# Scores of a two-branch encoder: a head's two maps alternate on the halves of TensorE's rows, and a 64-row product is padded with zeros to 128 rows

## The chip, the cores and the metric

The kernel runs on one core of one Trainium2 chip. The metric is device time of one execution in microseconds (us), the median of three runs. TensorE (PE) multiplies, VectorE (DVE) and ScalarE (ACT) do the elementwise work, GpSimd (POOL) and SyncE (SP) mostly issue transfers.

## The reference

Two encoder layers over 256 tokens of 2048 features, float32. Per layer, with `h = rmsnorm(x)`:

```
# differential attention, 8 heads, two maps c per head, 64 dims each
scores = einsum('bqhcd,bkhcd->bhcqk', qb, kh) * scale
probs = softmax(scores)
weights = probs[:, :, 0] - lam * probs[:, :, 1]
...
# latent attention, 8 heads: 128 plain dims, and 64 rotated dims whose key all heads share
scores = (einsum('bqhd,bkhd->bhqk', qn, k_nope) + einsum('bqhr,bkr->bhqk', qr, k_rope)) * scale
probs = softmax(scores)
...
x = x + (sigmoid(ga) * y_diff + sigmoid(gb) * y_mla) @ w_out
x = x + swiglu(rmsnorm(x))
x = x + sigmoid(rmsnorm(x) @ w_ple_gate) * (p @ w_ple_in)
```

The rest of the layer is matrix products with 2048 x 2048 or larger weights.

## The kernel before

Every operand of a product is held in two parts: the leading bits (`hi`) and the exact rest (`lo`); three products of parts make one product of values. The tokens lie along the free axis, 256 of them, so an operand tile is [128 features, 256 leading | 256 rest]. Weights come from HBM in pieces of up to 8 blocks of 128 x 128 (`piece`): SP issues the load, ACT writes `whi`, DVE writes `wlo`, and PE uses both; three buffers of each exist. A large product (`emit`) does per 128 features one matmul of 512 columns and one of 256 (L199, L200), or three of 256 (L195 to L197).

Scores are made by `scores` (L317 to L322) in a PSUM bank `S` of [128 queries, 2 query blocks, 256 keys]; `ps_s` has two banks. For each query block the query part is the stationary operand and the key part streams 256 columns, for the three pairs of parts that `three` lists. In the differential branch the two maps of a head share a tile: map 0 on partitions 0 to 63, map 1 on 64 to 127, so a matmul uses 64 of the array's 128 rows: 12 of them per head, 6 for each map (`diff_weights`). In the latent branch (`mla_weights`) a score block is three matmuls on all 128 rows (`qn`, `kn`) and three on 64 rows (`qr`, `kr`): two heads share a `qr` tile, one on each half of the partitions, and the shared rotated key `kr` lies twice in its tile, once on each half. So a latent head is 3 + 3 + 3 + 3 matmuls, 6 of them on 64 rows.

`exps` then takes the bank: DVE finds the row maxima (L327), ACT the exponents (L330) and DVE the inverse sums. The heads are pipelined: the weights of head h+1 are traced before the output of head h, and between them stand steps of other products (`beside`, or the first gates). The order on each engine is not that of the source: the Tile scheduler orders instructions by its own timeline simulation when the program is built, so the pieces of a score block can lie apart, with rows of other products between them.

Of the kernel before, what the change touches and what calls it, by code (L numbers as in the profile page):

```python
# [12 lines left out]
F32 = mybir.dt.float32  # L13
F32R = mybir.dt.float32r
# [5 lines left out]
P = 128  # L20
# [30 lines left out]
def encoder(ctx, tc, x, p, positions, cols, lams, wq, wk, wv, wcq, wckv, wkr, wga, wgb,  # L51
# [27 lines left out]

    # Operands of products: [128 features, leading bits of 256 tokens | rest]  # L80
    ua = [const.tile([P, 2 * T], F32R, name=f"ua{j}") for j in range(NC)]
    ub = [const.tile([P, 2 * T], F32R, name=f"ub{j}") for j in range(NC)]

    # Memory of varied use: plain values (two chunks) or an operand
    def slot(name):
# [6 lines left out]

# [1 line left out]
    xT = const.tile([P, NC, T], F32, name="xT")  # L94
# [11 lines left out]

# [1 line left out]
    ident = const.tile([P, P], F32, name="ident")  # L108
# [48 lines left out]

# [1 line left out]
    def piece(src, n):  # L159
        """n blocks of 128 x 128 weights: the 12 leading bits, and the exact rest."""  # L160
        w = wts.tile([P, PT * P], F32, tag="w32", name="w32", bufs=W_BUFS)
        hi = wts.tile([P, PT * P], F32R, tag="whi", name="whi", bufs=3)
        lo = wts.tile([P, PT * P], F32R, tag="wlo", name="wlo", bufs=3)
        m = n * P
        dst = w[:, :m]
        if len(src.shape) == 3:
            dst = dst.rearrange("p (a b) -> p a b", a=src.shape[1])
        nc.sync.dma_start(dst, src)
        last_split[:] = A.activation(hi[:, :m], w[:, :m], AF.Copy), tt(lo[:, :m], w[:, :m], hi[:, :m].bitcast(F32), ALU.subtract)  # L169
        if chores:  # L170
            with after_splits():
                chores.pop(0)()
        return hi, lo
# [10 lines left out]
    def after_splits():  # L184
        """What is traced inside comes behind the weights' splits so far, on their engines."""
        stack = ExitStack()
        for i in last_split:
            stack.enter_context(tc.issue_after(i.ins))
        return stack
# [12 lines left out]
    def product(src, us, whole=False):  # L202
        """A 128-column tile of a weight times the operands: [128, one part of the sum | the other],
        or, with more instructions, the whole sum in the first half."""
        acc = bank(ps_mm, "mm", "mm")
        n = len(us)
        for a in range(0, n, PT):
            m = min(PT, n - a)
            hi, lo = piece(src[:, a * P : (a + m) * P], m)
            emit(acc, hi, lo, 0, us[a : a + m], a == 0, a + m == n, whole)  # L210
        return acc[:, :T] if whole else acc

    def pair(src, us, whole=False):
        """The products of two tiles with few operands."""
        n = len(us)
        hi, lo = piece(src.rearrange("n p m -> p n m"), 2 * n)
        for j in range(2):
            acc = bank(ps_mm, "mm", "mm")
            emit(acc, hi, lo, j * n, us, True, True, whole)
            yield acc[:, :T] if whole else acc  # L220
# [19 lines left out]
    def rsqrt(src, n, eps, width):  # L240
        """1 / sqrt(src / n + eps), by Newton's steps from the bits' halved exponent."""
        v, y, a = (stat.tile([P, 2 * DH], F32, tag="r" + s, name="r" + s, bufs=2)[:, :width] for s in "vya")
# [16 lines left out]
    def norm(sums, n):  # L259
        """The norm's factor by token, tokens along partitions; sums: squares to be summed over partitions."""  # L260
        s = bank()
        for j, a in enumerate(sums):
            for b in range(2):
                PE.matmul(s[:, b : b + 1], a[:, b * P : (b + 1) * P], ones[:, 0:1], start=j + b == 0, stop=j + b == len(sums))  # L264
        return rsqrt(s[:, 0:2], n, EPS, 2)

    def spread(col, copied=True):
        """The factors along the free axis, the same in each partition."""
        dg = stat.tile([P, 2, P], F32, tag="dg", name="dg", bufs=1)
# [10 lines left out]
    def normed(sums, one, two):  # L280
        """The norm's factors, with two products that run while they are computed."""
        got = [joined(one())]
# [7 lines left out]
    def stream(us, gain):  # L290
        """Collects the chunks of the residual stream as the next products' operands."""
        acc = squares()
# [10 lines left out]

    def rotated(a, c_, s_, o):
        r = bank()
# [4 lines left out]
        tt(a, a, t, ALU.add)  # L310
        split(o, a)

    def three(q, k):
        return [(q[:, :T], k[:, :T]), (q[:, :T], k[:, T:]), (q[:, T:], k[:, :T])]

    def scores(pairs):
        """Scores of both query blocks, the products of the pairs summed: [queries, block, keys]."""  # L317
        S = bank(ps_s, "S", "S", (P, 2, T))
        for b in range(2):
            for j, (q, k) in enumerate(pairs):  # L320
                PE.matmul(S[:, b, :], q[:, b * P : (b + 1) * P], k, start=j == 0, stop=j == len(pairs) - 1)  # L321
        return S  # L322

    def exps(S, E, scale):
        """Exponents less the rows' maxima, and the inverse of their sums."""
        nm, sm, rs = (stat.tile([P, 2], F32, tag=t, name=t, bufs=4) for t in ("nm", "sm", "rsum"))
# [7 lines left out]
    def turned(W, parts=False):  # L334
        """W [queries, block, keys] as [keys, block, queries], plain or in two parts"""
        tp = bank(shape=(P, 2, T))
# [19 lines left out]
    def values(src, us, load=None):  # L356
        """Products with tokens on partitions [tokens, block, columns], by steps; the last gives them."""
        vals = stat.tile([P, 2, 2, 512], F32, tag="vals", name="vals", bufs=1)
# [22 lines left out]

# [1 line left out]
    warm = bank()  # L383
# [8 lines left out]
    for L in range(DEPTH):  # L392
        # -- differential values, tokens on partitions
        steps = values(wv[L], ua, None if L else load)
# [25 lines left out]

        # -- differential queries and keys, by head [2 x 64 dims, leading bits of the tokens | rest]
        qk = [(ub[h], operand(fa(h, F32R))) for h in range(DH)]
# [10 lines left out]

        # -- latents and what comes of them
        cq, ckv = ub[8:12], ub[12:14]
        kr = stat.tile([P, 2 * T], F32R, tag="kr", name="kr", bufs=1)
        qn, kn, qr = [], [], ub[14:]
# [43 lines left out]
        def beside():  # L481
            """What fills the differential attention: two steps to a head."""
            for h in range(2, DH):
                if h < 6:
                    keys_up(2 * h - 4)
                elif h == 7:
                    rotated(copied(product(wkr[L, 0], ua, True)), crm, srm, kr)
                yield
# [28 lines left out]

        # -- differential attention
        fill = beside()
# [3 lines left out]
        def diff_weights(h):  # L523
            q, k = qk[h]
            E, r = [weights(), weights("E1")], []
            for c in range(2):
                d = slice(c * 64, (c + 1) * 64)
                r.append(exps(scores(three(q[d], k[d])), E[c], 0.125))
            ts(r[1], r[1], neg_lam[:, L : L + 1], None, ALU.mult)
# [18 lines left out]
        def settle(h0):  # L548
            """The norms of four heads' outputs, and these with features on partitions again."""
            rd = rsqrt(ssd[:, 2 * h0 : 2 * h0 + 8], P, SUB_EPS, 8)  # L550
# [23 lines left out]

        # -- latent attention
        oms = ub[8:]
        todo = iter(range(NC))

        def mla_weights(h):
            d = slice((h % 2) * 64, (h % 2) * 64 + 64)  # L580
            E = weights()
            r = exps(scores(three(qn[h], kn[h]) + three(qr[h // 2][d], kr[d])), E, MLA_SCALE)
            for b in range(2):
# [18 lines left out]

        # -- gates and branches, merged
        for n in range(NC):
# [17 lines left out]

        # -- SwiGLU
        R, _, pre = normed([acc], lambda: product(w_gate[L, 0], ub), lambda: product(w_up[L, 0], ub))
# [27 lines left out]

        # -- ple
        R, _, pre = normed([acc], lambda: product(w_pg[L, 0], ub), lambda: product(w_pg[L, 1], ub))
# [34 lines left out]
def rope_constants():  # L689
    """By partition: the frequency and the sine's sign for both kinds of rotation, and the  # L690
    exchange of a 64-wide block's halves."""
    c = np.zeros((P, 4 + P), np.float32)
# [13 lines left out]
def tiles(w):  # L706
    """[depth, K, N] -> [depth, N / 128, 128 of a K chunk, K chunks x 128 columns]"""
    d, k, n = w.shape
# [4 lines left out]
def wide(w):  # L713
    """[depth, K, N] -> [depth, N / 512, 128 of a K chunk, K chunks x 512 columns]"""
    d, k, n = w.shape
# [51 lines left out]
```

## Time and profile before

| | us |
|---|---|
| median of three runs | 2960.72 |
| lowest, highest | 2960.64, 2961.24 |
| span of the profiled execution, first to last instruction | 2958.3 |
| PE busy in it | 2941.5 |
| DVE busy, ACT busy | 2039.6, 1519.9 |

The profiled execution's own time is given as its span; the timed runs add some 2.4 us around it. In a list of instructions in order of time, a row gives the start and the length of a group, and "64*128" is the part of the array that a matmul uses (rows * columns). Matmuls are pipelined, so their lengths overlap: what one costs PE is the distance from its start to the next one's start, not its length. In the program, 17273 matmuls stand on PE, of which 384 are scores.

### The profile page before, as it was taken

The numbers are of one execution on the slowest core, as the hardware profiler recorded it, in microseconds if no ns is written. First come the engines' busy times: TensorE is split into PE (matmuls) and PEld (weight loads), VectorE is DVE, ScalarE is ACT, GpSimd is POOL, SyncE is SP. The second block draws the span as 40 slices with busy tenths as digits, with TensorE's granted clock in tenths as the row PEclk, the third lists the DMA queues.
The fourth block names the chain that finished last, engine by engine and source line by source line (L and its number), as shares of the span: only waits on it lengthen the run. The fifth ranks groups of instructions, "written<-read, shape, count | busy, mean of one in ns | idle before, by whom it ended". The sixth has DMA issues, their size and how long they took to land.

```text
span 2958.3 us, 45148 instructions
## 1 busy us (share of the span) xinstructions
PE 2941.5 (99%) x17390; PEld 2592.0 (88%) x17390; DVE 2039.6 (69%) x3445; ACT 1519.9 (51%) x2510; POOL 2.5 (0%) x9
## 2 busy tenths in 40 slices
PE   9999999999999999999999999999999999999998
PEld 7998888888888888888889988888888888888887
DVE  7887657776666656667858875587666666566676
ACT  6666545554444444444646755455444444444554
POOL 0000000000000000000000000000000000000000
PEclk9999999999999999999999999999999999999999
DMA  6444456555565566566554444565556655655654
GB/s 231 159 153 140 150 186 192 188 186 186 182 194 187 175 195 193 187 188 187 186 186 157 150 137 158 189 189 187 186 189 183 191 189 179 194 189 187 187 186 141
DMA packets 155751, 532.47 MB, mean 180 GB/s; under 512 B 16928, under 2 KB 23584, under 8 KB 155536
## 3 DMA queue, kind: packets, MB, share of 16 engines
q1 hardware_dynamic: 154944, 528.55, 56.2%
q8 instruction: 136, 2.23, 0.3%
q0 software_dynamic: 160, 0.46, 0.1%
q14 instruction: 79, 0.65, 0.1%
q10 hardware_dynamic: 432, 0.59, 0.1%
HBM read 527.43 MB, written 2.10 MB: 179 GB/s over the span
## 4 chain that ended last, share of the span: by engine, by line
PE 99%; DVE 0%; DMA 0%; SPq 0%; ACT 0%; issue 0%; DVEq 0%
PE mm L199 55%; PE mm L200 29%; PE mm L197 3%; PE mm L195 3%; PE mm L196 3%; PE S L321 2%; PE mmv L372 1%; PE mmv L374 1%; PE mmv L373 1%; PE at L339 1%; PE at L541 0%; PE at L598 0%; DMA w<-in_wv 0%; PE at L273 0%; PE at L306 0%; PE at L264 0%
## 5 line engine op out<-in xcount | busy, mean ns | idle before, releaser
L72 DVE TENSOR_TENSOR wlo<-w,whi 128x1024 fp32r<-128x1024 f32 (+2 forms) x1029 | 1229.1, 1194 | 788.3 <-ACT whi L169 776.4
L169 ACT ACTIVATE whi<-w 128x1024 fp32r<-128x1024 f32 (+2 forms) x1029 | 1066.0, 1036 | 1339.2 <-issue 781.7
L199 PE MATMUL mm<-ub,whi 128*128 128x512 f32 x3920 | 1379.3, 394 | 0.0
L200 PE MATMUL mm<-ub,wlo 128*128 128x256 f32 x3920 | 1109.2, 283 | 0.0
L199 PE MATMUL mm<-ua,whi 128*128 128x512 f32 x3136 | 1104.7, 394 | 0.0
L200 PE MATMUL mm<-ua,wlo 128*128 128x256 f32 x3136 | 886.1, 283 | 0.0
L199 PEld LDWEIGHTS mm<-ub,whi 128*128 128x128 f32 x3920 | 736.1, 188 | 169.6
L200 PEld LDWEIGHTS mm<-ub,wlo 128*128 128x128 f32 x3920 | 737.0, 188 | 0.2
L199 PEld LDWEIGHTS mm<-ua,whi 128*128 128x128 f32 x3136 | 588.4, 188 | 132.6
L200 PEld LDWEIGHTS mm<-ua,wlo 128*128 128x128 f32 x3136 | 589.6, 188 | 1.6
L197 PE MATMUL mm<-ua,wlo 128*128 128x256 f32 x608 | 173.0, 285 | 0.0
L195 PE MATMUL mm<-ua,whi 128*128 128x256 f32 x608 | 172.6, 284 | 0.0
L196 PE MATMUL mm<-ua,whi 128*128 128x256 f32 x608 | 172.3, 284 | 0.0
L72 DVE TENSOR_TENSOR a<-mm,join 128x256 f32<-128x256 f32 x371 | 154.6, 417 | 0.5 <-ACT join L229 0.2
L72 DVE TENSOR_TENSOR xT<-xT,mm 128x256 f32<-128x256 f32 x256 | 106.7, 420 | 51.8 <-PE mm L200 47.9
L229 ACT ACTIVATE join<-mm 128x256 f32<-128x256 f32 x371 | 136.1, 367 | 3.8 <-PE mm L200 3.8
L197 PEld LDWEIGHTS mm<-ua,wlo 128*128 128x128 f32 x608 | 114.5, 188 | 1.6
L195 PEld LDWEIGHTS mm<-ua,whi 128*128 128x128 f32 x608 | 114.6, 188 | 1.3
L196 PEld LDWEIGHTS mm<-ua,whi 128*128 128x128 f32 x608 | 114.6, 188 | 0.5
L72 DVE TENSOR_TENSOR a<-a,row 128x256 f32<-128x256 f32 x207 | 87.3, 424 | 6.6 <-ACT row L277 0.8
L372 PE MATMUL mmv<-whi,ua 128*128 128x512 f32 x128 | 51.5, 402 | 2.2 <-ACT whi L169 2.2
L72 DVE TENSOR_TENSOR a<-a 128x256 f32<-128x256 f32 x120 | 51.0, 425 | 4.0
(161 smaller groups left out, 1514.1 us busy)
## 6 DMA issues: line engine op xcount, KB each, us to landing
w<-in_w_gate SPq DMA_DIRECT2D x176, 512.0 KB, 4.5
w<-in_w_up SPq DMA_DIRECT2D x176, 512.0 KB, 4.5
w<-in_w_down SPq DMA_DIRECT2D x128, 512.0 KB, 4.1
w<-in_wga SPq DMA_DIRECT2D x64, 512.0 KB, 3.7
w<-in_wgb SPq DMA_DIRECT2D x64, 512.0 KB, 4.5
w<-in_w_out SPq DMA_DIRECT2D x64, 512.0 KB, 4.4
w<-in_w_pg SPq DMA_DIRECT2D x64, 512.0 KB, 4.4
w<-in_w_down SPq DMA_DIRECT2D x64, 384.0 KB, 3.5
```

Of the source, the lines that this page charges most:

```text
L72: return V.tensor_tensor(out=o, in0=a, in1=b, op=op)
L169: last_split[:] = A.activation(hi[:, :m], w[:, :m], AF.Copy), tt(lo[:, :m], w[:, :m], hi[:, :m].bitcast(F32), ALU.subtract)
L195: PE.matmul(acc[:, :T], hi[:, s], u[:, :T], start=start, stop=False)
L196: PE.matmul(acc[:, :T], hi[:, s], u[:, T:], start=False, stop=False)
L197: PE.matmul(acc[:, :T], lo[:, s], u[:, :T], start=False, stop=stop)
L199: PE.matmul(acc, hi[:, s], u, start=start, stop=False)
L200: PE.matmul(acc[:, T:], lo[:, s], u[:, :T], start=False, stop=stop)
L229: A.activation(t, acc[:, T:], AF.Copy)
L321: PE.matmul(S[:, b, :], q[:, b * P : (b + 1) * P], k, start=j == 0, stop=j == len(pairs) - 1)
L339: PE.transpose(tp[:, kb, b * P : (b + 1) * P], W[:, b, kb * P : (kb + 1) * P], ident)
L372: PE.matmul(banks[b], xh, hi[:, s], start=a + j == 0, stop=False)
L373: PE.matmul(banks[b], xl, hi[:, s], start=False, stop=False)
```

## The change

Four things are edited. `scores` takes any number of maps: it takes a bank for each at once, and inside a query block it issues for each pair of parts first map 1, then map 0, so a differential head's 12 matmuls alternate between the halves of the rows. `three` lists the pair of both leading parts last instead of first. The single tile `kr` becomes two, `krs[0]` with the key on partitions 0 to 63 and `krs[1]` with it on 64 to 127; the other half is set to zero by POOL once at the start. `rotated` writes the key's two halves into the two tiles, in four operations of 64 partitions instead of two of 128. `mla_weights` uses all 128 rows of the shared `qr` tile against `krs[h % 2]`; the zeros cancel the other head's half. To make room, the memory for dynamic DMA is given as 8192 bytes.

```
+    krs = [const.tile([P, 2 * T], F32R, name=f"kr{j}") for j in range(2)]
+    for t in krs:
+        nc.gpsimd.memset(t.bitcast(F32), 0.0)
+
-    def rotated(a, c_, s_, o):
+    def rotated(a, c_, s_, o=None):
...
-        split(o, a)
+        if o is None:
+            for j, t in enumerate(krs):
+                split(t[64 * j : 64 * j + 64], a[64 * j : 64 * j + 64])
+        else:
+            split(o, a)
 
     def three(q, k):
-        return [(q[:, :T], k[:, :T]), (q[:, :T], k[:, T:]), (q[:, T:], k[:, :T])]
-
-    def scores(pairs):
-        S = bank(ps_s, "S", "S", (P, 2, T))
+        return [(q[:, :T], k[:, T:]), (q[:, T:], k[:, :T]), (q[:, :T], k[:, :T])]
+
+    def scores(*maps):
+        Ss = [bank(ps_s, "S", "S", (P, 2, T)) for _ in maps]
         for b in range(2):
-            for j, (q, k) in enumerate(pairs):
-                PE.matmul(S[:, b, :], q[:, b * P : (b + 1) * P], k, start=j == 0, stop=j == len(pairs) - 1)
-        return S
+            for j in range(len(maps[0])):
+                for S, pairs in reversed(list(zip(Ss, maps))):
+                    q, k = pairs[j]
+                    PE.matmul(S[:, b, :], q[:, b * P : (b + 1) * P], k, start=j == 0, stop=j == len(pairs) - 1)
+        return Ss
...
-        kr = stat.tile([P, 2 * T], F32R, tag="kr", name="kr", bufs=1)
...
-                    rotated(copied(product(wkr[L, 0], ua, True)), crm, srm, kr)
+                    rotated(copied(product(wkr[L, 0], ua, True)), crm, srm)
...
-            E, r = [weights(), weights("E1")], []
-            for c in range(2):
-                d = slice(c * 64, (c + 1) * 64)
-                r.append(exps(scores(three(q[d], k[d])), E[c], 0.125))
+            E = [weights(), weights("E1")]
+            halves = [slice(c * 64, (c + 1) * 64) for c in range(2)]
+            r = [exps(S, e, 0.125) for S, e in zip(scores(*(three(q[d], k[d]) for d in halves)), E)]
...
-            d = slice((h % 2) * 64, (h % 2) * 64 + 64)
             E = weights()
-            r = exps(scores(three(qn[h], kn[h]) + three(qr[h // 2][d], kr[d])), E, MLA_SCALE)
+            S, = scores(three(qn[h], kn[h]) + three(qr[h // 2], krs[h % 2]))
+            r = exps(S, E, MLA_SCALE)
...
-    nc = bacc.Bacc("TRN2", target_bir_lowering=False, num_devices=1)
+    nc = bacc.Bacc("TRN2", target_bir_lowering=False, num_devices=1, dynamic_dma_scratch_size=8192)
```

The built programs show where the scheduler puts the rows. On PE in layer 0, the scores of the fourth differential head (fa3, ub3; `mm` rows are a weight product, `S_1761` is map 0's bank and `S_1776` map 1's) stand before like this:

```order
L196 MATMUL mm_1873<-ua3_79,whi_1875 128x256
L321 MATMUL S_1761<-fa3_586,ub3_95 128x256
L321 MATMUL S_1776<-fa3_586,ub3_95 128x256
L197 MATMUL mm_1873<-ua3_79,wlo_1876 128x256
L195 MATMUL mm_1873<-ua4_80,whi_1875 128x256
```

and, four `mm` rows later:

```order
L197 MATMUL mm_1873<-ua5_81,wlo_1876 128x256
L321 MATMUL S_1761<-fa3_586,ub3_95 128x256 x5
L321 MATMUL S_1776<-fa3_586,ub3_95 128x256 x5
L195 MATMUL mm_1873<-ua6_82,whi_1875 128x256
```

In the changed program the same head (`S_1765` is map 1's bank, `S_1764` map 0's) stands so; the two S rows shown repeat until there are twelve:

```order
L352 MATMUL at_1799<-ident_112,E_1543 128x128 x3
L334 MATMUL S_1765<-fa3_590,ub3_95 128x256
L334 MATMUL S_1764<-fa3_590,ub3_95 128x256
L334 MATMUL S_1765<-fa3_590,ub3_95 128x256
L334 MATMUL S_1764<-fa3_590,ub3_95 128x256
```

Two pieces of 2 and 10 matmuls, one map after the other, have become one piece of 12 that alternates. Six of a layer's eight heads become one piece. The first head stays in pieces of 7 and 5 around a row of L273. The last head, two pieces of 2 and 10 before, now stands on PE in three (at_2668 is a transpose, at_2694 the rotation's product):

```order
L334 MATMUL S_2726<-fa7_594,ub7_99 128x256
L567 MATMUL at_2668<-ident_112,fa3_2170 128x128 x2
L334 MATMUL S_2725<-fa7_594,ub7_99 128x256
L334 MATMUL S_2726<-fa7_594,ub7_99 128x256
L334 MATMUL S_2725<-fa7_594,ub7_99 128x256
L312 MATMUL at_2694<-a_2692,rc_110 128x256
L334 MATMUL S_2726<-fa7_594,ub7_99 128x256
```

The pieces are of 5, 3 and 4 matmuls. Counted over both layers, the 64-row matmuls of the differential branch lie in 34 pieces before and in 22 after; those of the latent branch in 36 pieces before, and after there are none, since all its rows are 128 rows wide.

The third place is PE in layer 0 at the third and fourth latent heads. Before, the third is a whole and the fourth comes much later:

```order
L306 MATMUL at_2896<-a_2894,rc_110 128x256
L541 MATMUL at_2904<-vals_138,wt_2852 128x128 x4
L321 MATMUL S_3298<-fb2_1527,fa2_2824 128x256 x3
L321 MATMUL S_3298<-kr_591,ub15_107 128x256 x3
L321 MATMUL S_3298<-fb2_1527,fa2_2824 128x256 x3
L321 MATMUL S_3298<-kr_591,ub15_107 128x256 x3
L372 MATMUL mmv_3054<-whi_3057,ub12_104 128x512
```

In the changed program the fourth head's bank follows the third's at once:

```order
L387 MATMUL mmv_3038<-wlo_3041,ub13_105 128x512
L334 MATMUL S_3303<-fb2_1530,fa2_2829 128x256 x3
L334 MATMUL S_3303<-kr0_129,ub15_107 128x256 x3
L334 MATMUL S_3303<-fb2_1530,fa2_2829 128x256 x3
L334 MATMUL S_3303<-kr0_129,ub15_107 128x256 x3
L312 MATMUL at_2901<-a_2899,rc_110 128x256
L552 MATMUL at_2909<-vals_142,wt_2857 128x128 x4
L334 MATMUL S_3449<-fb3_1540,fa3_2845 128x256 x3
L334 MATMUL S_3449<-kr1_130,ub15_107 128x256 x3
```

The fourth head's scores have moved forward, to 17 matmuls behind the third's start. `S_3449` needs the bank that the second head used (`S_3157`), so it comes behind that head's exponents. On ACT these now stand behind the split of a weight piece:

```order
L343 ACTIVATE E_3081,sm_3096<-S_3082,nm_3095 128x256 x2
L169 ACTIVATE whi_3108<-w32_3107 128x1024
L229 ACTIVATE join_3030<-mm_3020 128x256
L354 ACTIVATE wt_2857<-at_2852 128x512
L169 ACTIVATE whi_3130<-w32_3129 128x1024
L343 ACTIVATE E_3156,sm_3171<-S_3157,nm_3170 128x256 x2
```

`whi_3130` takes the buffer of the piece that the `mmv_3038` matmuls read, so it waits for the last of them, which stands just ahead of the third head's scores. Elsewhere the engines keep their rows: SP issues the same transfers in the same order, PE has 17273 matmuls as before, DVE and ACT have two instructions more each in all, POOL two.

## Rows read from the trace of the kernel before

**Rows 1.** The page: busy times, engines of the chain that ended last, one group.

```profile
PE 2941.5 (99%) x17390; PEld 2592.0 (88%) x17390; DVE 2039.6 (69%) x3445; ACT 1519.9 (51%) x2510; POOL 2.5 (0%) x9
...
PE 99%; DVE 0%; DMA 0%; SPq 0%; ACT 0%; issue 0%; DVEq 0%
...
L169 ACT ACTIVATE whi<-w 128x1024 fp32r<-128x1024 f32 (+2 forms) x1029 | 1066.0, 1036 | 1339.2 <-issue 781.7
```

**Rows 2.** Tile S: count, ns least/median/most, first and last start (us), forms.

```profile
L321 PE MATMUL S<-fa,ub x192: 271/278/384, 113.1 to 1691.4; 64*128 64x256 f32 x192
L330 ACT ACTIVATE E<-S,nm x96: 453/467/498, 119.5 to 1813.4; 128x256 f32<-128x256 f32 x96
...
L321 PE MATMUL S<-fb,fa x96: 276/281/471, 230.5 to 1807.8; 128*128 128x256 f32 x96
L327 DVE TENSOR_REDUCE nm<-S x48: 678/682/693, 114.1 to 1809.1; 128x2 f32<-128x512 f32 x48
...
L321 PE MATMUL S<-kr,ub x48: 272/330/385, 234.7 to 1749.5; 64*128 64x256 f32 x48
...
L321 PE MATMUL S<-kr,fc x48: 274/279/387, 297.2 to 1808.4; 64*128 64x256 f32 x48
```

**Rows 3.** PE in order of time, fourth differential head: start, length (us), matmul, count.

```profile
155.85 0.28 PE L195 MATMUL mm<-ua,whi 128*128 128x256 f32 x1
155.97 0.28 PE L196 MATMUL mm<-ua,whi 128*128 128x256 f32 x1
156.18 0.39 PE L321 MATMUL S<-fa,ub 64*128 64x256 f32 x2
156.50 0.39 PE L197 MATMUL mm<-ua,wlo 128*128 128x256 f32 x1
156.72 0.28 PE L195 MATMUL mm<-ua,whi 128*128 128x256 f32 x1
156.84 0.28 PE L196 MATMUL mm<-ua,whi 128*128 128x256 f32 x1
...
157.53 1.08 PE L321 MATMUL S<-fa,ub 64*128 64x256 f32 x10
158.54 0.39 PE L195 MATMUL mm<-ua,whi 128*128 128x256 f32 x1
```

**Rows 4.** PE in order of time, a latent head.

```profile
311.28 0.51 PE L321 MATMUL S<-fb,fa 128*128 128x256 f32 x3
311.72 0.62 PE L321 MATMUL S<-kr,fc 64*128 64x256 f32 x3
312.27 0.62 PE L321 MATMUL S<-fb,fa 128*128 128x256 f32 x3
312.82 0.62 PE L321 MATMUL S<-kr,fc 64*128 64x256 f32 x3
313.37 0.33 PE L339 MATMUL at<-ident,E 128*128 128x128 f32 x1
```

**Rows 5.** PE in order of time, rotated rows of two latent heads.

```profile
234.69 0.51 PE L321 MATMUL S<-kr,ub 64*128 64x256 f32 x4
235.12 0.38 PE L541 MATMUL at<-vals,wt 128*128 128x128 f32 x1
```

**Rows 6.** PE in order of time, the first differential head.

```profile
113.14 0.97 PE L321 MATMUL S<-fa,ub 64*128 64x256 f32 x7
114.03 0.70 PE L273 MATMUL at<-dg,ones 128*128 128x256 f32 x2
```

**Rows 7.** PE in order of time, the seventh differential head, second and third piece.

```profile
202.61 0.85 PE L321 MATMUL S<-fa,ub 64*128 64x256 f32 x6
203.39 0.70 PE L306 MATMUL at<-a,rc 128*128 128x256 f32 x2
204.02 0.74 PE L321 MATMUL S<-fa,ub 64*128 64x256 f32 x4
204.69 0.33 PE L339 MATMUL at<-ident,E 128*128 128x128 f32 x1
```

## The prediction

> **What bounds the kernel now.** I read the page first, then the tile of the scores, then PE in order of time around the scores. On the page PE is busy 99% of the span and the chain that ended last is PE to 99%, so DVE (69%) and ACT (51%) only matter where they make PE wait [rows 1]. A microsecond off PE's own sequence is a microsecond off the end, as long as the order that replaces it finds its operands ready.
>
> The scores are 384 matmuls: 192 of the differential maps on 64 rows, 96 latent ones on 128 rows, 48 + 48 rotated ones on 64 rows [rows 2]. Their listed lengths (about 0.28 us) overlap and say little; the distances between starts say what they cost.
>
> **What a 64-row matmul costs.** In the fourth head the weight product's 256-column matmuls start 0.12 us apart (155.85 to 155.97, 156.72 to 156.84). The first 64-row matmul comes 0.21 after the one before it (155.97 to 156.18) and not 0.12: entering costs 0.09. The matmul behind the piece keeps the next one 0.22 away (156.50 to 156.72): leaving costs 0.10. Between them the piece of two, one of each map, takes 0.32 from its start to the next matmul's (156.18 to 156.50) [rows 3]. Four rotated matmuls, two of one head on the lower half and two of the next head on the upper, take 0.43 (234.69 to 235.12) [rows 5]. So a second pair adds 0.11, about what one full-width matmul costs, and two matmuls on different halves run at once. A piece of n pairs therefore costs 0.09 + 0.10 + 0.32 + 0.11 (n - 1). The fixed part, about 0.4 us for going to 64 rows and back, is more than three matmuls' worth.
>
> The piece of ten in that head takes 1.01 (157.53 to 158.54) [rows 3], where five pairs would take 0.32 + 4 x 0.11 = 0.76: with five of one map and then five of the other in the program, PE overlaps some but not all.
>
> **The differential heads.** The built order gives the pieces, and the formula what they cost; all of it is PE time.
> - Second to sixth head of each layer: before 0.19 + 0.32 + 0.19 + 1.01 = 1.71; after one piece of six pairs, 0.19 + 0.32 + 5 x 0.11 = 1.06. Gain 0.65 each, 3.25 per layer.
> - Seventh head: the first piece is a pair as in the others, 0.32, the other two take 0.78 (202.61 to 203.39) and 0.67 (204.02 to 204.69) [rows 7]; with three times 0.19 that is 2.34. After, 1.06. Gain 1.28.
> - First head: the piece of seven takes 0.89 (113.14 to 114.03) [rows 6]; alternating it is three pairs and a single, 0.32 + 3 x 0.11 = 0.65. The piece of five, all of one map, is 0.32 + 4 x 0.12 = 0.80 and becomes 0.54. Gain 0.50.
> - Last head: before 1.71 by the same two pieces; after, pieces of 5, 3 and 4 are 0.54 + 0.43 + 0.43 and three times 0.19, 1.97. Loss 0.26.
>
> Sum per layer 3.25 + 1.28 + 0.50 - 0.26 = 4.77, for both 9.5 us.
>
> **The latent heads.** In the head shown, three full-width matmuls between two rotated pieces take 0.55 (312.27 to 312.82) where 3 x 0.12 = 0.36: leaving one piece and entering the next costs 0.19. A rotated piece of three itself takes 0.55 (311.72 to 312.27) instead of 0.36 [rows 4]. So each piece costs 0.19 + 0.19 = 0.38 over what the same matmuls cost at full width, whether it holds one matmul or four, since the fixed part does not depend on the number. There are 36 such pieces over both layers, and after there is none: 36 x 0.38 = 13.7. What is given up are the pairs that already ran side by side, as in [rows 5]: two there and one in a later piece of three, six over both layers, 6 x 0.11 = 0.7. Net 13.0 us. The zeros cost nothing on PE: a full-width matmul of 256 columns keeps its 0.12 whatever lies in its rows, by the first piece of the same head (311.28 to 311.72 is 3 x 0.12 and the entry's 0.09) [rows 4].
>
> The Trainium skill speaks against this half: TensorEngine Tiling (Array Packing), section Performance Considerations, recommends splitting the rows in two where the contraction is 64 or less, and its overview promises up to twice the speed. By that rule the 96 rotated matmuls would cost half a slot each before, and the padding would lose 96 x 0.06 = 5.8 us. The trace does not bear it out here, because a head's rotated matmuls all lie on one half and follow one another.
>
> **Work on other engines.** Writing the key's halves adds one ACT and one DVE operation per layer; they are off the chain [rows 1] and stand well ahead of the first latent scores, so I cost them at nothing. If that cover were gone, it would be under 1 us a layer. Two zero fills are new on POOL, whose nine instructions take 2.5 us together [rows 1]; they stand at the start and are needed only for the first layer's latent part, 200 us later. The small DMA memory serves three early transfers; nothing. Listing the leading parts' pair last makes a score block start only once the key's rest is written by DVE; the scheduler places it behind that, which is why the piece is whole.
>
> **New waits.** The fourth latent head's scores stand 17 matmuls behind the third's start and need the second head's bank. Its release takes a weight split of 1.04 us [rows 1] and two exponents of 0.47 [rows 2], 1.98 in all, from the end of the matmuls just ahead of the third head. PE in the meantime has twelve full-width matmuls (1.43), the rotation's product (203.39 to 204.02 less 0.19, 0.44) [rows 7] and four more matmuls. That covers it, barely, so I take zero; with no cover at all, and the maximum search of 0.68 late as well [rows 2], it would be 2.7 a layer. Behind these scores the values' and gates' products are queued on PE, so such a wait would go straight to the end.
>
> **Sum.** 9.5 + 13.0 = 22.5 us off the profiled execution's span of 2958.3, so 2935.8; the runs' median lies 2.4 above the span, hence 2960.7 - 22.5 = 2938.2 us.
>
> **Rivals.**
> - *The waits come back.* The moved scores of the latent heads, or a score block that needs both banks at once, wait for ACT at one place a layer: 2 x 2.7 = 5.4 us, time 2943.6. For it: the fourth head's cover is thin. Against: PE's waits are nowhere near 1% in the order that the same scheduler made before [rows 1]. Chance 0.09.
> - *No overlap in strict turns.* If a matmul on one half waited for the one just ahead on the other, a piece of twelve would be twelve slots. That is 46 slots a layer more than in the sum, 92 x 0.12 = 11.0, time 2949.2. For it: the piece of ten overlaps only in part [rows 3]. Against: pairs, and two pairs in a row, take the time of one and of two slots [rows 3, 5]. Chance 0.08.
> - *Padding loses.* Rotated matmuls at full width cost more than they did, 5.8 us by the reckoning above, with the differential gain kept: 2960.7 - 9.5 + 5.8 = 2957.0. Against: the 0.55 for three of them [rows 4]. Chance 0.02.
> - *Slower: the banks.* Both banks are filled together and come free only after two maximum searches and four exponents, 2 x 0.68 + 4 x 0.47 = 3.24 us [rows 2]. If the next head's scores waited all of that at the seven later heads of each layer, 14 x 3.24 = 45.4 us would come back, time 2983.6. It decides from 22.5 / 14 = 1.6 us a head. Against: in the built order the pieces of successive heads are at least 88 matmuls apart, over 10 us. Chance 0.03. The Trainium skill names the mechanism: TensorEngine Tiling (Array Packing), section PSUM Bottleneck, warns that row tiling speeds up TensorE but not the reading of its banks. No run here shows it yet.
>
> **How the numbers follow.** The forecast has 0.78. It could come out better where the hidden second weight load of an alternating piece makes entering cheaper: at 22 pieces 0.1 us, 2.2, and little else; 2935 is about the floor, and I put the low end at 2934. The high end must take in the waits and the lost overlap, 2950. A change under 0.2% (5.9 us) can't be told from none in this kernel: so faster is all of the forecast and of the first two rivals, 0.95; within 0.2% is the padding rival and a partial bank wait, 0.03; slower 0.02.
>
> **What would show it.** In the profile after: full-width rows only in latent heads, the three-and-three groups starting 0.36 apart; a differential piece of twelve taking about 0.87 from its start to the next matmul; matmuls on PE unchanged at about 17390 records, PE still 99% of the chain. The forecast is wrong if the piece of twelve takes 1.4 or more (no overlap), or if PE shows idle time before S with ACT or DVE named as releaser (waits), or if padded matmuls start more than 0.12 apart.

## The result, and the profile after

The changed kernel took 2939.99 us (median of 4 runs, 2938.37 to 2941.0) against 2960.98 for the kernel before beside it (4 runs, 2960.64 to 2962.35): a ratio of 0.9929, 95% interval 0.9917 to 0.9941. That is 21.0 us less, where 22.5 were predicted. The profiled execution's span went from 2958.3 to 2937.4 us, 20.9 less.

The page of the changed kernel: busy times and the engines of the chain that ended last.

```profile
PE 2918.8 (99%) x17390; PEld 2583.1 (88%) x17390; DVE 2039.8 (69%) x3447; ACT 1520.5 (52%) x2512; POOL 3.5 (0%) x11
...
PE 99%; DVE 0%; DMA 0%; ACT 0%; SPq 0%; issue 0%; DVEq 0%
```

PE has the same 17390 records and is 22.7 us less busy; the chain is still PE to 99%, and the other engines have kept their work [rows 1]. Tile S on PE, its four groups (count, least, median and most ns, first and last start in us, form):

```profile
L334 PE MATMUL S<-fa,ub x192: 271/277/387, 114.6 to 1677.8; 64*128 64x256 f32 x192
L334 PE MATMUL S<-fb,fa x96: 277/283/366, 230.8 to 1787.7; 128*128 128x256 f32 x96
L334 PE MATMUL S<-kr,ub x48: 274/281/286, 231.2 to 1698.9; 128*128 128x256 f32 x48
L334 PE MATMUL S<-kr,fc x48: 280/283/285, 290.6 to 1788.1; 128*128 128x256 f32 x48
```

The counts are those of before, and the 96 rotated matmuls are now 128 rows wide [rows 2]. Their lengths would mislead: 64-row and 128-row matmuls are all listed with about 280 ns. The distances between starts tell what changed. PE in order of time in the fourth differential head of the changed kernel (start, length in us, matmul, count):

```profile
155.80 0.28 PE L196 MATMUL mm<-ua,whi 128*128 128x256 f32 x1
155.91 0.28 PE L197 MATMUL mm<-ua,wlo 128*128 128x256 f32 x1
156.04 0.49 PE L352 MATMUL at<-ident,E 128*128 128x128 f32 x3
156.46 0.97 PE L334 MATMUL S<-fa,ub 64*128 64x256 f32 x12
157.36 0.39 PE L195 MATMUL mm<-ua,whi 128*128 128x256 f32 x1
157.58 0.28 PE L196 MATMUL mm<-ua,whi 128*128 128x256 f32 x1
```

Two pieces of 0.32 and 1.01 us [rows 3] have become one of 0.90 (156.46 to 157.36), and PE pays once, not twice, for going to 64 rows and back; the exit still keeps the next matmul 0.22 away (157.36 to 157.58). The same view of a latent head:

```profile
303.90 0.28 PE L200 MATMUL mm<-ua,wlo 128*128 128x256 f32 x1
304.02 0.52 PE L334 MATMUL S<-fb,fa 128*128 128x256 f32 x3
304.38 0.52 PE L334 MATMUL S<-kr,fc 128*128 128x256 f32 x3
304.74 0.52 PE L334 MATMUL S<-fb,fa 128*128 128x256 f32 x3
305.10 0.52 PE L334 MATMUL S<-kr,fc 128*128 128x256 f32 x3
305.45 0.49 PE L352 MATMUL at<-ident,E 128*128 128x128 f32 x3
```

Each three take 0.36 us. The twelve take 1.43, against 2.09 before (311.28 to 313.37) [rows 4]. The three pieces of the last differential head:

```profile
220.44 0.62 PE L334 MATMUL S<-fa,ub 64*128 64x256 f32 x5
220.99 0.44 PE L567 MATMUL at<-ident,fa 128*128 128x128 f32 x2
221.35 0.50 PE L334 MATMUL S<-fa,ub 64*128 64x256 f32 x3
221.78 0.70 PE L312 MATMUL at<-a,rc 128*128 128x256 f32 x2
222.41 0.50 PE L334 MATMUL S<-fa,ub 64*128 64x256 f32 x4
222.84 0.50 PE L199 MATMUL mm<-ub,whi 128*128 128x512 f32 x1
```

**The sum over all pieces.** For each piece I took the distance from the last matmul before it to the second one after it, less what its neighbours usually need (the extra time; the piece's own matmuls are in it, and for the latent scores a piece is the rotated matmuls alone, before and after). For the differential scores it was 29.2 us in 34 pieces before and is 20.2 in 22 pieces; for the latent scores it was 24.7 and is 11.4. That is 9.0 and 13.2 us less, 22.3 together. From the first score to the start of the last pair of matmuls the trace gives the same: 2948.33 - 113.14 = 2835.19 before, and 2927.49 - 114.63 = 2812.86 after, 22.3 less.

**The 1.5 us that the span lacks** lie ahead of the first scores, in the wait of the values' first steps. What PE waits for in the changed kernel (engine, line, releaser; us in total, times, longest):

```profile
PE mmv L385 <- ACT whi L169: 4.2, 2, 3.1
PE at L273 <- DVE dg L78: 2.7, 1, 2.7
PE at L264 <- ACT ssq L253: 2.0, 1, 2.0
PE at L398 <- DVE ones L111: 1.1, 1, 1.1
```

and in the kernel before:

```profile
PE at L273 <- DVE dg L78: 2.7, 1, 2.7
PE mmv L372 <- ACT whi L169: 2.2, 3, 1.0
PE at L264 <- ACT ssq L253: 2.0, 1, 2.0
PE at L385 <- DVE ones L111: 1.1, 1, 1.1
```

No wait for scores, exponents or banks has come. The only longer one is the values' third step, which in the changed kernel's profile starts here:

```profile
6.65 0.62 PE L387 MATMUL mmv<-wlo,ua 128*128 128x512 f32 x2
10.32 0.50 PE L385 MATMUL mmv<-whi,ua 128*128 128x512 f32 x1 [3.06 <-ACT whi L169]
```

ACT in turn stood there 3.5 us for a transfer of x. In the profile of before the same matmul waited 0.54:

```profile
9.27 0.50 PE L372 MATMUL mmv<-whi,ua 128*128 128x512 f32 x1 [0.54 <-ACT whi L169]
```

So the first scores start at 114.63 and not at 113.14 [rows 6]. Whether the change does this, three of the runs below ask.

### The profile page after: what moved, and what is told of

Read it like the earlier page. It is cut to its first block, busy times and chain, and to the rows that moved or that the text cites. A ratio compares the mean times of both kernels' runs of the same rounds, so it can differ in the third digit from the quotient of the medians.

```text
span 2937.4 us, 45159 instructions
## 1 busy us (share of the span) xinstructions
PE 2918.8 (99%) x17390; PEld 2583.1 (88%) x17390; DVE 2039.8 (69%) x3447; ACT 1520.5 (52%) x2512; POOL 3.5 (0%) x11
## 4 chain that ended last, share of the span: by engine, by line
PE 99%; DVE 0%; DMA 0%; ACT 0%; SPq 0%; issue 0%; DVEq 0%
PE mm L199 56%; PE mm L200 29%; PE mm L195 3%; PE mm L197 3%; PE mm L196 3%; PE S L334 1%; PE mmv L385 1%; PE mmv L386 1%; PE mmv L387 1%; PE at L352 0%; PE at L552 0%; PE at L609 0%; DMA w<-in_wv 0%; PE at L273 0%; DVE xT L72 0%; PE at L312 0%
```

## The experiments

They ran in three groups on three chips, each beside runs of the kernel before (medians 2960.45, 2960.68 and 2961.32). The edits are shown against the changed kernel, except small_scratch's, which is against the kernel before, and paired's, which is against pinned; "..." marks lines left out. The theory under test is the prediction's: a stretch of 64-row matmuls costs about 0.4 us for its two ends whatever its length, and inside it alternating halves run two to a slot.

**The padding alone (pad_only).** The differential maps follow one another as before, and `three` lists the pairs of parts as before.

```
-        return [(q[:, :T], k[:, T:]), (q[:, T:], k[:, :T]), (q[:, :T], k[:, :T])]
+        return [(q[:, :T], k[:, :T]), (q[:, :T], k[:, T:]), (q[:, T:], k[:, :T])]
...
-            E = [weights(), weights("E1")]
-            halves = [slice(c * 64, (c + 1) * 64) for c in range(2)]
-            r = [exps(S, e, 0.125) for S, e in zip(scores(*(three(q[d], k[d]) for d in halves)), E)]
+            E, r = [weights(), weights("E1")], []
+            for c in range(2):
+                d = slice(c * 64, (c + 1) * 64)
+                r.append(exps(scores(three(q[d], k[d]))[0], E[c], 0.125))
```

> Only the latent half of the change: the rotated key padded with zeros, the differential heads' maps one after the other and the pairs of parts listed as before, so the differential pieces stand on PE as before (17 a layer) and the latent branch has no 64-row matmul. Theory (each going to 64 rows and back costs PE a fixed 0.4 us): 36 pieces x 0.38 less 0.7 us of lost overlap, about 13 us faster than before, near 2948, and the latent rows 0.12 us apart throughout. Rival (the gain comes from the new order and the whole differential pieces, padding is neutral): under 3 us. Rival (padding costs 96 half slots): about 6 us slower than before.

Measured: 2948.17 us (2947.35 to 2949.43), ratio 0.9959 [0.9944, 0.9974], 12.3 less than before. The differential heads' extra time stayed at 29.2 us, so all of this is the latent part. The rivals that padding loses, and that it is neutral (under 3 us), are out.

**The turns alone (turns_only).** The key keeps one tile, written as before, the rotated part its 64 rows, and the DMA memory its old size.

```
...
-            S, = scores(three(qn[h], kn[h]) + three(qr[h // 2], krs[h % 2]))
+            S, = scores(three(qn[h], kn[h]) + three(qr[h // 2][d], kr[d]))
...
```

> Only the differential half: maps in turns, pairs of parts in the new order, one key tile, rotated latent rows on 64 rows. The differential pieces are those of the changed kernel (11 a layer), the latent branch has 14 pieces of 64 rows a layer where it had 18. Theory: 9 us from the differential heads, and 8 latent pieces fewer x 0.38 less 0.7 us of lost overlap, 2.3 us; in all about 11 us faster than before, near 2950. Rival (no overlap in strict turns, the gain of the changed kernel is the padding's alone): 2 us faster or less.

Measured: 2952.02 us (2950.87 to 2952.65, 8 runs), 0.9971 [0.996, 0.9982], 8.4 less. I had expected about 11, because I counted the latent pieces of this build as 28; there are 34, and their extra time is that of before, 24.7 us. With the right count the theory says about 9 less. The differential heads' extra time fell from 29.2 to 20.2, as in the changed kernel. A latent head in this kernel's trace still has the slow rotated rows:

```profile
307.06 0.51 PE L326 MATMUL S<-fb,fa 128*128 128x256 f32 x3
307.50 0.62 PE L326 MATMUL S<-kr,fc 64*128 64x256 f32 x3
```

The two halves alone are worth 12.3 and 8.4, together 20.7; the change is worth 21.0. They add.

**One piece without turns (no_turns).** The same pieces at the same places, but map 1's six matmuls and then map 0's.

```
-        for b in range(2):
-            for j in range(len(maps[0])):
-                for S, pairs in reversed(list(zip(Ss, maps))):
-                    q, k = pairs[j]
+        for S, pairs in reversed(list(zip(Ss, maps))):
+            for b in range(2):
+                for j, (q, k) in enumerate(pairs):
```

> The changed kernel with the same pieces in the same places, but inside a piece all six matmuls of map 1 and then all six of map 0. Theory (PE overlaps matmuls on different halves only where they stand near each other in the program; ten rows 5 + 5 took 7 slots in the kernel before): a piece of twelve takes 8 or 9 slots, 1.10 to 1.24 us to the next matmul instead of 0.88, in all 5 to 6.5 us slower than the changed kernel, near 2946. Rival (strict order, only the last of one map and the first of the other overlap): 11 slots, 9 us slower or more. Rival (PE reorders freely, turns bring nothing): within 1 us of the changed kernel.

Measured: 2945.51 us (2945.07 to 2947.42), 0.9951 [0.9936, 0.9966], 5.5 more than the changed kernel, which was timed beside other runs of before (by the ratios it is 6.5). From the first score to the last pair of matmuls it needs 6.0 more. A piece of twelve in its trace:

```profile
173.31 0.28 PE L196 MATMUL mm<-ua,whi 128*128 128x256 f32 x1
173.52 1.31 PE L333 MATMUL S<-fa,ub 64*128 64x256 f32 x12
174.77 0.39 PE L197 MATMUL mm<-ua,wlo 128*128 128x256 f32 x1
```

It takes 1.25 us against 0.90: about nine slots, neither the eleven of strict order nor the six of turns. So of the differential heads' gain some 3 us come from having fewer pieces (extra time 29.2 to 26.2) and 6 from the turns (26.2 to 20.2).

**The differential scores at full width (diff_full).** Same matmuls, same order, no 64-row form; each map then holds the sum of both maps' products, which is not what the reference computes.

```
-            halves = [slice(c * 64, (c + 1) * 64) for c in range(2)]
+            halves = [slice(0, P) for c in range(2)]
```

> The changed kernel with the same rows in the same order on every engine, but the differential scores use all 128 rows: each map then holds the sum of both maps' products, so the output is not the reference's. No matmul of the kernel changes the width then. Theory (fixed 0.4 us a piece for the change of width, 0.12 a full-width matmul): a head's twelve take 1.43 in place of 1.06, but the split first and last head lose their pieces' fixed cost; +1.3 us a layer, 2.7 us slower than the changed kernel, near 2942.5, and a score block's first matmul comes 0.12 after the row before it. Rival (the fixed cost belongs to the start of a score block, its new bank or operands, and not to the width): 22 pieces keep 0.4 us, some 11 us slower than the changed kernel.

Measured: 2941.67 us (2941.2 to 2943.91), 0.9938 [0.9924, 0.9953], 1.7 more than the changed kernel (by the ratios, 0.9938 - 0.9929, it is 2.7). The fourth head in its trace:

```profile
156.30 0.49 PE L352 MATMUL at<-ident,E 128*128 128x128 f32 x3
156.55 1.65 PE L334 MATMUL S<-fa,ub 128*128 128x256 f32 x12
158.04 0.28 PE L195 MATMUL mm<-ua,whi 128*128 128x256 f32 x1
158.16 0.28 PE L196 MATMUL mm<-ua,whi 128*128 128x256 f32 x1
```

The entry's and exit's delays are gone (158.04 to 158.16 is 0.12), but the twelve take 1.49. From the first score to the last pair of matmuls this kernel needs 2.7 us more than the changed one, exactly the theory's number, and its first scores came at 114.32. The rival, by which the fixed cost belongs to the start of any block of scores, wanted a time some 11 us above the changed kernel's and is out. Using the halves at all is worth only 2.7 of the 22 us: a whole piece saves six slots of 0.12 (0.7 us) and pays 0.4 for its ends, and the heads that stand in two or three pieces pay those more than once.

**Does the change start later? (after_again, small_scratch, late_fill.)** Three runs on one chip: the changed kernel once more; the kernel before with only the smaller DMA memory; and the changed kernel with the zero fills moved off the start.

> The changed kernel itself, for times beside the next three on one chip: near 2940, the first scores at 114 to 116 us where the kernel before has 113.1.

```
-    nc = bacc.Bacc("TRN2", target_bir_lowering=False, num_devices=1)
+    nc = bacc.Bacc("TRN2", target_bir_lowering=False, num_devices=1, dynamic_dma_scratch_size=8192)
```

> The kernel before, with the memory for dynamic DMA at 8192 bytes and nothing else changed; all engines keep their rows. The four traces with the padded key reach their 25th value matmul at 16.0 to 17.4 us, the two without at 14.9 and 15.2. Theory A (the small memory delays the first transfers): that matmul at 16 us or later, time 1 to 2 us above the kernel before. Theory B (the zero fills on POOL do it): 14.9 to 15.2 us, time unchanged. Theory C (the arrival of the first transfers varies from run to run): either, and no difference in the medians.

```
     def lambdas():
+        for t in krs:
+            V.memset(t.bitcast(F32), 0.0)
...
-    for t in krs:
-        nc.gpsimd.memset(t.bitcast(F32), 0.0)
```

> The changed kernel with the two zero fills on DVE, some 30 us into the program, instead of on POOL at the start. Theory B (POOL's fills at the start delay the first transfers): the 25th value matmul at about 15 us, time about 1.3 us under the changed kernel. Theories A and C: no difference beyond the spread of the runs, under 0.5 us.

Measured: 2939.16 us (2938.69 to 2940.92), 0.9927 [0.9913, 0.9941]; 2960.82 (2960.05 to 2963.4, 11 runs), 1.0001 [0.9992, 1.001]; 2939.46 (2939.17 to 2941.1), 0.9928 [0.9915, 0.994]. Neither edit moves the time by more than the runs' spread. The same place in the profile of small_scratch, whose program is that of before but for the memory's size:

```profile
6.63 0.64 PE L374 MATMUL mmv<-wlo,ua 128*128 128x512 f32 x2
9.29 0.50 PE L372 MATMUL mmv<-whi,ua 128*128 128x512 f32 x1 [2.03 <-ACT whi L169]
```

Here the wait is 2.03, against 0.54 in before, with an unchanged median, so the start varies from execution to execution: over all profiles the first scores come between 113.1 and 117.5 us. The zero fills do not cause it (2939.46 without them at the start). Whether the changed kernel starts later on average, by the 1 us that lies between 22.3 and the medians' 21.0 and 21.5, the few profiles cannot tell; that stays open. Some of that 1 us may be no start at all: in small_scratch's profile the stretch from the first score to the last pair of matmuls is 2834.79, 0.4 less than in that of before.

**Sixteen whole pieces (pinned).** The first and last head's pieces are kept together too, by keeping the first matmul of each block behind what the program has ahead of it.

```
-                    PE.matmul(S[:, b, :], q[:, b * P : (b + 1) * P], k, start=j == 0, stop=j == len(pairs) - 1)
+                    i = PE.matmul(S[:, b, :], q[:, b * P : (b + 1) * P], k, start=j == 0, stop=j == len(pairs) - 1)
+                    if b + j == 0 and len(maps) == 2 and S is Ss[1]:
+                        tc.keep_in_program_order(i)
```

> The changed kernel with the first matmul of each differential head queued behind the PE row traced before it, which makes the first and the last head of a layer one piece each: 16 pieces of twelve where there were 22. Theory (a piece costs 0.4 us fixed): the first head's two pieces 1.60 become 1.09, the last head's three 1.96 become 1.09, 1.4 us a layer, 2.7 us faster than the changed kernel, near 2937. Rival (the last head's scores, now 17 rows later on PE, make the transposes of its weights wait): the gain is spent on PE idle time before L352, no faster or up to 3 us slower.

> The pinned kernel once more, for times beside the next one on the same chip: near 2936.

Measured: 2935.85 us (2935.66 to 2936.1), 0.9915 [0.9901, 0.9928], 3.3 less than after_again on the same chip, where 2.7 was expected (from the first score to the last pair of matmuls it is 3.7); and on the third chip 2936.61 (2935.94 to 2937.74), 0.9917 [0.9904, 0.9931]. The ranges don't overlap with the changed kernel's. The first head in its trace is now whole:

```profile
114.30 0.59 PE L273 MATMUL at<-dg,ones 128*128 128x256 f32 x2
114.83 0.97 PE L334 MATMUL S<-fa,ub 64*128 64x256 f32 x12
115.73 0.38 PE L196 MATMUL mm<-ub,whi 128*128 128x256 f32 x1
```

With 16 pieces the extra time is 17.4 us, after 29.2 with 34 and 20.2 with 22: the last six pieces cost 0.47 us each. PE's waits have no new row, so the rival of late transposes is out. This kernel beats both.

**Turns for the rotated rows too (paired).** Two latent heads' blocks are made together; their rotated rows take turns on the halves, with one key tile, without zeros, and with a third buffer for the exponents. On top of pinned:

```
...
+            for b in range(2):
+                for j in range(3):
+                    for c in (1, 0):
+                        d = slice(c * 64, c * 64 + 64)
+                        q, k = three(qr[h // 2][d], kr[d])[j]
+                        i = PE.matmul(got[c][:, b, :], q[:, b * P : (b + 1) * P], k, start=False, stop=b + j == 3)
+                        tc.keep_in_program_order(i)
...
```

> The pinned kernel with the other way to treat the latent heads: one key tile without zeros, two heads' score blocks made together, their rotated rows on 64 rows in turns between the halves. On PE 5 pieces a layer hold the 48 rotated rows. Theory (a piece 0.40 us and 0.11 a pair, a full-width matmul 0.12): 48 x 0.12 = 5.76 at full width against 5 x 0.40 + 25 x 0.11 = 4.75, 1.0 us a layer, 2 us faster than the pinned kernel, near 2934. Rival (both banks of scores are filled together and must both be read before the next two heads: PE idles before L592 on ACT): the gain is spent, 2936 or more. Rival (padding is the better way, a pair of heads in turns costs as much as before's pieces): 3 us slower or more.

Measured: 2938.9 us (2938.34 to 2941.34), 0.9927 [0.9914, 0.9939], 2.3 more than pinned beside it. A pair of heads in its trace, and then three of its waits on PE that pinned does not have:

```profile
319.86 1.58 PE L592 MATMUL S<-fb,fa 128*128 128x256 f32 x12
321.38 0.98 PE L598 MATMUL S<-kr,fc 64*128 64x256 f32 x12
322.29 0.66 PE L346 MATMUL at<-ident,E 128*128 128x128 f32 x4
```

```profile
PE at L308 <- ACT wt L348: 1.4, 2, 0.7
...
PE at L547 <- DVE sh L72: 1.0, 2, 0.5
PE S L592 <- ACT E L337: 0.6, 2, 0.3
```

The twelve rotated matmuls do take 0.91 us and not 1.43, and the extra time of the latent scores falls by 1.9 us. Against that stand 3.0 us of new waits, all at one place in each layer. The same place in order of time:

```profile
240.91 0.70 PE L308 MATMUL at<-a,rc 128*128 128x256 f32 x2 [0.69 <-ACT wt L348]
242.12 1.16 PE L547 MATMUL at<-vals,wt 128*128 128x128 f32 x8 [0.51 <-DVE sh L72]
243.58 0.98 PE L592 MATMUL S<-fb,fa 128*128 128x256 f32 x6 [0.31 <-ACT E L337]
```

The listed idle time is only part of the price. The two rotation matmuls take 1.21 us to the next row (240.91 to 242.12) where they take 0.43 in pinned (238.72 to 239.15), and the eight behind them take 1.46 (242.12 to 243.58) where they take 0.85 (239.15 to 240.00): 0.78 and 0.61 more, with 0.51 and 0.31 listed as idle behind them. From the first score to the last pair of matmuls paired needs 3.0 us more than pinned (2812.14 and 2809.13), so with 1.9 gained some 4.9 were lost. Its late start (first scores at 117.48 us) has no part in that; the medians, 2.3 apart, have each kernel's start in them.

Only the third wait, 0.6 us, is for a bank of scores, the rival that was named. The second is for DVE, which has the maximum searches of both banks to do one behind the other there (240.45 to 241.73) and the rotation's products behind them. The first is for ACT's copy of the transposes. In pinned the next head's scores stand between the transposes and the rotation on PE (237.19 to 238.72) and cover such work; in paired they have been made before. That this order causes all three waits is argued from it and not tested.

## Why the prediction was right

- **The bound.** PE's own sequence set the end; 22.3 us less of it between the first score and the last pair moved the end by 21 us. No other engine came up behind it.
- **The differential heads, 9.5 us predicted, 9.0 measured.** The piece of twelve takes 0.90 and not 0.87 (a pair within it adds nearly 0.12, not 0.11): 0.03 for each of 12 pieces is 0.4 of the 0.5 missing. The last head's three pieces take 0.55, 0.43 and 0.43 where 0.54, 0.43 and 0.43 were reckoned, so its loss was real, and pinned took it back. The formula's split into ends and slots is shown by no_turns (same ends, 9 slots for 6 in a whole piece: 5.5 us more) and diff_full (no ends, twelve slots: 2.7 us more).
- **The latent heads, 13.0 predicted, 13.2 measured,** and 12.3 in the time of pad_only. Padded matmuls start 0.12 apart as all full-width ones do. The rival weighed against this half, that padding loses, failed for the reason given: a short stretch of one head on one half pays both ends and overlaps nothing. In paired, where twelve take turns, the rotated matmuls on 64 rows were cheaper than padded ones by 1.9 us, before the waits.
- **New waits at zero.** The fourth latent head's scores follow without idle time on PE; the cover that was barely enough held. The zero fills on POOL took 0.54 us each and cost nothing (late_fill).
- **The span.** 1.5 us of it went to a later start, which the prediction had no term for, and which varies between executions. The 2.4 us that it adds from span to time were 1.95 in the changed kernel's profiled run (2939.35 and 2937.4); the two offset each other in part.
- **The range.** The cheaper way into an alternating piece, which the low end allowed for, did not come: the step is 0.21 in the changed kernel (for one, 130.33 to 130.54), as before. And a change under 0.2% can be told from none in this kernel: pinned, 0.1% below the changed kernel, shares no time with it.
- **The rivals.** Waits that come back: no such row among PE's waits. No overlap in strict turns: 0.90 for twelve where 1.4 was its mark. Padding loses: pad_only. Slower by banks: not with heads so far apart; where paired puts two together, 0.6 us of such a wait shows.

## What to carry to other kernels

Count the stretches of half-height matmuls, not the matmuls: each stretch costs about 0.4 us at its two ends here, and only matmuls on different halves close to each other earn it back, 0.12 us for each pair that runs together; strict alternation pairs them all, six and then six paired half (nine slots for twelve). By these two figures, a stretch of fewer than four pairs, or of one half alone, is better padded with zeros to full height, where the operands allow it; long ones should be kept whole and alternating, even against the scheduler (pinned). Before pairing more work, look at what the other engines then have to do at once: gathering two heads' scores saved 1.9 us on PE and brought waits that cost more.

## What the runs showed of the hardware

- PE seems not to wait strictly for its turn. In no_turns the program has six matmuls on one half and then six on the other, with one place where neighbours differ, and yet the twelve take nine slots, with three starts 8 ns or less behind another (for one, 173.862 and 173.869). That fits PE beginning matmuls of the second half some rows ahead of their place; the records don't name the half, so this is inferred from the starts. It would also explain the piece of ten before, 1.01 us where strict order would need nine slots [rows 3]. The Trainium skill, page TensorE: Matmul & The Clock Gate, Part 3: Packing small matmuls, says that matmuls start and end in strict program order, without reordering; these starts differ from that, and here the measurement decides.
- Beside 256-column rows of a weight product, the two ends of a stretch cost the same in every kernel here: 0.21 from the matmul before (173.31 to 173.52 in no_turns) and 0.22 after it (157.36 to 157.58 in the changed kernel), where 0.12 is usual. The Trainium skill, page TensorEngine Tiling (Array Packing), section Key Properties, says that a change of tiling mode drains the engine; the trace agrees, in that these delays are gone in diff_full, where the width never changes, and it gives their price.
- The start varies from one execution to the next. The first scores came at 114.63 and 116.16 us in two executions of the changed kernel, and at 113.14 and 115.70 in two of kernels that differ only in the size of the DMA memory, with the same median time. In these profiles PE waits early on for ACT, and ACT for transfers of x and of the values' weights. A difference of 1 or 2 us between two single spans means little until the start is taken out.
